# Silu as one ScalarE instruction, an early table load, folded ALiBi distances and moved tile addresses in a two-layer mLSTM and NSA decoder

## The chip, the core and the metric

The kernel runs on one NeuronCore of a Trainium2 chip. A core has engines that each run their own queue of instructions in order: TensorE (PE in the profile; its weight loads are PEld), VectorE (DVE), ScalarE (ACT), GpSimd (POOL) and SyncE (SP, which here only issues DMAs). They meet through semaphores. The metric is device microseconds of one execution; three executions of the kernel before took 578.73, 580.31 and 580.7 us, so its time is the median, 580.31 us.

## The reference

All data are float32; a sequence of 256 tokens, width 1024, two layers. Layer A is an mLSTM, layer B attends sparsely over keys and values that are computed once between the layers.

```python
def mlstm_mixer(h, w_in, conv_w, conv_b, w_q, w_k, w_v, w_gate, b_gate, head_norm, skip, w_out):
    xm, o_pre, z = jnp.split(h @ w_in, 3, axis=-1)          # 1024 -> 3 x 2048
    xc = jax.nn.silu(causal_depthwise_conv(xm, conv_w, conv_b))   # 4 taps
    q, k, v = blockdiag(xc, w_q), blockdiag(xc, w_k), blockdiag(xm, w_v)   # 512 blocks of 4 x 4
    gates = q @ w_gate[:2048] + k @ w_gate[2048:4096] + v @ w_gate[4096:] + b_gate
    cell = mlstm_cell(heads(q), heads(k), heads(v), i_pre, f_pre)    # 4 heads of 512
    hc = sigmoid(heads(o_pre)) * cell
    hn = per-head layer norm of hc, times head_norm
    return ((hn + skip * xc) * silu(z)) @ w_out

def nsa_mixer(h, kv, w_in, w_out):        # 16 heads of 128 in 2 groups, 3 branches
    q = (h @ w_q) * 128 ** -0.5
    s = q @ k.T - slopes[head] * distance     # masked where distance < 0
    p = masked_softmax(s, mask)               # for each of the 3 branches
    o = sum over branches of sigmoid(gate) * silu(z_branch) * (p @ v)
    return o @ w_out

x = x + rmsnorm(mixer(rmsnorm(x, g_pre)), g_post)      # for both layers
```

The three branches are the compressed blocks (15 of them, computed by a small MLP), the selected blocks and the window; at 256 tokens the last two see all earlier tokens.

## The kernel before, in words

The kernel is written for a framework that works out each engine's order when the program is built, from the order of the code, priorities (`high_priority`) and explicit hints (`issue_after(ins)`, meaning that an instruction is put behind `ins` on its engine). Tiles come from pools with a fixed number of buffers, and an instruction that needs a buffer still in use waits.

*Products in three passes.* Each float32 operand is split into a high part, a copy rounded to `fp32r`, and a low part, the rest. `split` makes the high part on ScalarE (L134, `whi<-raw`) and the low part on VectorE (L135, `wlo<-raw,whi`). `mm3` issues three matmuls: high x high, high x low, low x high (L139 to L141); the third is the one that needs the low half of the weights. `weights` (L117 and after) loads a tile of 128 x 1024 weights by a DMA from SP's queue (L123) into `raw` (4 buffers) and splits it into `whi` (5 buffers) and `wlo` (4). `proj_t` multiplies two such tiles with the normalised input `hA` (layer A) or `hB` (layer B); it gives a transposed result of 256 features by 256 tokens.

*Layer A up to the gates (some 12 to 95 us).* The loop at L364 goes over j = 0 to 7, 256 features each. In each turn it runs `proj_t` into `xmps`, copies it to `xm` (L373, ScalarE), starts the convolution with the fourth tap and the bias on ScalarE (`conv`, L378), adds three taps for each of the two feature tiles on VectorE (L381, six instructions), and applies Silu as conv * (1 + tanh(conv / 2)): Tanh on ScalarE (`th`, L384), then one VectorE instruction (`xc`, L385). The factor 0.5 that is missing so far, `xc` being twice the Silu, is put into its users: the gate weights (L354), the scores (L504: 0.25), the vector that holds `skip` (L305: 0.25 instead of 0.5). Between the projections stand quarters of the output gates (`o_gate`, L322). In the turns j = 4 and 5 `gate_product` (L345 to L354) makes the weights `wgt` of the gates, products of the 4 x 4 blocks with the gate matrix. Then `gps2` and `gps` (L398 and after) give the gates from `xm` and `xc`, and a chain of small steps on 4 rows follows, among them Abs, Exp and Ln on ScalarE (L421 to L423).

*Cells.* `block_product` (L356 to L360, called at L560) makes M, the blocks of w_q times w_k transposed. `cell_scores` expands the blocks to 128 x 128 tiles `bd` on GpSimd (L472), which wait for M; it makes the scores and the values `v`. `z_gate`, `cell_out` and `cell_y` follow for each head, then the output projection `OutProj` (its sums are `acc`; the weight tiles of its last steps are `wl`).

*Keys and values, and layer B (250 us to the end).* `wv` holds weights of the values; `dist` (L647 and after) holds the distances of every query to every key of all branches, MASKED = 1e33 where a key is not seen. Then heads run in pairs, p = 0 to 7: `q_proj` (L809) scales q and splits it; `softmaxes` (L817) makes `al` = -slope * dist on GpSimd (L825, one pass over 128 x 800 per head), scores on TensorE (`sps`), then on VectorE score + `al` with the row maximum (L838), the negated maximum `nm` (L841), and on ScalarE Exp with that bias (L846). `z_branch` makes silu(z) of a branch from `zps`; `transposes` turns the softmax results (`pt`, and `ptc` for the compressed branch, L886); `values` (L903) multiplies them with the values and writes y, for the pairs 0 to 3 into `ylow`, a tile that uses the buffer of a former input, for the others into tiles of the pool `yp`. The second `OutProj` ends the program.

Of the kernel before, what the change touches and what calls it, by code (L numbers as in the profile page):

```python
# [7 lines left out]
F32 = mybir.dt.float32  # L8
# [7 lines left out]
P = 128  # L16
# [4 lines left out]
def trunk(ctx: ExitStack, tc: tile.TileContext, x, norm_pre, norm_post, a_w_in, a_conv_w, a_conv_b,  # L21
# [171 lines left out]
    def new_hT(name):  # L193
        return [hp.tile([P, KT, S], F32R, tag="h8", name=f"{name}_{s}") for s in ("hi", "lo")]
# [51 lines left out]
    with ExitStack() as actx:  # L246
# [5 lines left out]

        NF = AI // P
# [22 lines left out]
        with tc.issue_after(last_pow[0].ins):  # L276
# [28 lines left out]
            nc.vector.tensor_scalar(vec[:, 96:112], vps[:, 96:112], 0.25, None, op0=ALU.mult)  # L305
# [39 lines left out]
        def gate_product(a):  # L345

            terms = ((wq_row, wg[0]), (wk_row, wg[1])) if a == 0 else ((blk[:, 1], wg[2]),)
            pr = ys.tile([P, NF, 2 * AH, len(terms), 4], F32, tag="y4", name=f"prod{a}")
            for i, (r, w) in enumerate(terms):
                nc.vector.tensor_mul(pr[:, :, :, i, :], rows(r, 2 * AH), w.rearrange("p t (j c) -> p t c j", j=4))  # L350
            dst = wgt[:, a, :, 0:2 * AH]
            nc.vector.tensor_reduce(dst, pr, axis=AX.XY if len(terms) > 1 else AX.X, op=ALU.add)
            if a == 0:
                nc.vector.tensor_scalar(dst, dst, 0.5, None, op0=ALU.mult)  # L354
# [9 lines left out]
        for j in range(NF // 2):  # L364
            if j > 1:
                next(og[(j - 2) // 4])
            with ExitStack() as st:
                if j > 0:
                    st.enter_context(tc.issue_after(last_mm[0]))
                ps = proj_t(a_w_in[0], j * 256, hT, "xmps")  # L370
            hold.clear()
            h, j0 = divmod(2 * j, HT)
            nc.scalar.activation(xm[h][:, j0:j0 + 2, 3:], ps, AF.Copy)  # L373
            acc = a2.tile([P, 2, S], F32, tag="conv", name="conv")
            for m in range(2):
                f = 2 * j + m
                src = xm[h][:, j0 + m, :]
                nc.scalar.activation(acc[:, m, :], src[:, 3:], AF.Identity, scale=vec[:, 48 + f:49 + f],  # L378
                                     bias=vec[:, 64 + f:65 + f])
                for k in range(3):  # L380
                    nc.vector.scalar_tensor_tensor(acc[:, m, :], src[:, k:k + S], vec[:, 16 * k + f:16 * k + f + 1],  # L381
                                                   acc[:, m, :], op0=ALU.mult, op1=ALU.add)
            th = a2.tile([P, 2, S], F32, tag="th", name="th")
            nc.scalar.activation(th, acc, AF.Tanh, scale=0.5)  # L384
            nc.vector.scalar_tensor_tensor(xc[h][:, j0:j0 + 2, :], th, 1.0, acc, op0=ALU.add, op1=ALU.mult)  # L385
            if j in (4, 5):
                gate_product(j - 4)
        next(og[1])
# [80 lines left out]
        def cell_scores(h):  # L469
# [34 lines left out]
            nc.vector.scalar_tensor_tensor(dd, sps, 0.25 * ADH ** -0.5, dd, op0=ALU.mult, op1=ALU.mult)  # L504
# [55 lines left out]
        block_product()  # L560
# [24 lines left out]
        for c in range(4):  # L585
# [7 lines left out]
            vch.append([a.rearrange("p (k n) -> p k n", k=2) for a in hl])  # L593
        hK = new_hT("hK")
# [27 lines left out]
    with ExitStack() as bctx:  # L622
# [25 lines left out]
        for c0, base in ((0, 0), (P + NB, 0), (W0, 0), (W0 + P, P), (W0 + 2 * P + NB, P), (W0 + 3 * P + NB, 0)):  # L648
            seg = dist[:, c0:c0 + P]
            nc.gpsimd.iota(seg, pattern=[[-1, P]], base=base, channel_multiplier=1,  # L650
                           allow_small_or_imprecise_dtypes=True)
            if base == 0:
                nc.gpsimd.affine_select(out=seg, in_=seg, pattern=[[-1, P]], compare_op=ALU.is_ge,
                                        fill=MASKED, base=0, channel_multiplier=1)
        for c0, base in ((P, 0), (W0 + 2 * P, P)):
            seg = dist[:, c0:c0 + NB]
            nc.gpsimd.iota(seg, pattern=[[-16, NB]], base=base, channel_multiplier=1,
                           allow_small_or_imprecise_dtypes=True)
            nc.gpsimd.tensor_scalar(seg, seg, -15.5, None, op0=ALU.add)
            nc.gpsimd.affine_select(out=seg, in_=seg, pattern=[[-16, NB]], compare_op=ALU.is_ge,  # L660
                                    fill=MASKED, base=base - 31, channel_multiplier=1)
# [147 lines left out]
        def q_proj(p):  # L809
            ps = proj_t(bw, p * 256, hB, "qps")  # L810
            q = [qz.tile([P, 2, S], F32R, tag=f"q{s}", name=f"q{s}{p}") for s in ("hi", "lo")]
            sc = float(DK) ** -0.5
            nc.scalar.activation(q[0], ps, AF.Copy, scale=sc)
            nc.vector.scalar_tensor_tensor(q[1], ps, sc, q[0].bitcast(F32), op0=ALU.mult, op1=ALU.subtract)
            return q

        def softmaxes(p, q):  # L817
# [3 lines left out]
            for j in range(2):  # L821
                h = 2 * p + j
                al = b2.tile([P, W0 + KW], F32, tag="al", name=f"al{h}")
                with tc.issue_after(after_norm):
                    nc.gpsimd.tensor_scalar(al, dist, -slopes[h], None, op0=ALU.mult)  # L825
                e = E[:, j, :]
                mx = col(6, "mx")
                for t in range(NT):
# [7 lines left out]
                    for b, (c0, n) in enumerate(segs[t]):  # L836
                        src = next(s[:, c0 - o:c0 - o + n] for o, w, s in where if o <= c0 < o + w)
                        nc.vector.tensor_tensor_reduce(e[:, c0:c0 + n], src, al[:, c0:c0 + n], 1.0, -1e30,  # L838
                                                       ALU.add, ALU.max, mx[:, 3 * t + b:3 * t + b + 1])
                nm = col(6, "nm")  # L840
                nc.vector.tensor_scalar(nm, mx, -1.0, None, op0=ALU.mult)  # L841
                sm = col(6, "sm")
                for t in range(NT):
                    for b, (c0, n) in enumerate(segs[t]):
                        i = 3 * t + b
                        nc.scalar.activation(e[:, c0:c0 + n], e[:, c0:c0 + n], AF.Exp, bias=nm[:, i:i + 1],  # L846
                                             accum_out=sm[:, i:i + 1])
# [55 lines left out]
        def values(p, pts, zz):  # L903
            ptc, pt0, pt1 = pts
            g = p // 4
            if p < 4:
# [63 lines left out]
        yp = bctx.enter_context(tc.tile_pool(name="yp", bufs=8, reuse_waits="tile"))  # L970
        ylow = [hp.tile([P, 4, 2, S], F32R, tag="h8", name=f"ylow{s}") for s in ("hi", "lo")]
# [60 lines left out]
```

## Time and profile before

| | |
|---|---|
| three executions | 578.73, 580.31, 580.7 us (median 580.31) |
| profiled execution | 581.31 us |
| its span in the trace | 579.5 us |
| granted TensorE clock over it | 0.998 |
| busy: TensorE, VectorE, ScalarE, GpSimd | 97%, 78%, 54%, 16% |
| time from turn to turn in layer B, per pair of heads | 28.5 us |

The rows that follow come from one execution, recorded by the hardware profiler. A busy share is an average over the whole program; where an engine stands still, and for whom, is read from the lists of waits and the timelines. A wait is put down to the event that ended last before the instruction began.

### The profile page before, as it was taken

What the parts mean: (1) busy time and instruction counts of PE and PEld (TensorE: products, weight loads), DVE (VectorE), ACT (ScalarE), POOL (GpSimd) and SP (SyncE); (2) the same over time, 40 slices, a digit from 0 to 9 for tenths busy, and PEclk for the clock granted to TensorE, in tenths of its full rate; (3) what the DMA queues carried; (4) which work ended last, traced back from release to release, by engine and by line L of the source; (5) the groups of instructions that cost most, each with busy time, mean ns of one, the idle gap of its engine ahead of it and who ended that gap; (6) DMA issues with size and microseconds to landing.
All of it is one profiled execution on the core that took longest, in us unless ns stands there. A gap on an engine that the chain in (4) does not pass through costs nothing.

```text
span 579.5 us, 10616 instructions
## 1 busy us (share of the span) xinstructions
PE 563.6 (97%) x4043; PEld 511.6 (88%) x4043; DVE 451.1 (78%) x944; ACT 310.7 (54%) x585; POOL 90.1 (16%) x104
## 2 busy tenths in 40 slices
PE   7988999999999999999999999999999999999995
PEld 3977986898999988879899999999999999998884
DVE  7679887485898886777625789989978989998663
ACT  5464775545454435563424574747474747475521
POOL 7610000201020040130003112121211221200000
PEclk9999999999999999999999999999999999999999
DMA  8985664344314347779896553636374636354601
GB/s 262 223 246 177 218 192 140 107 146 146 114 48 131 112 156 241 224 261 280 265 316 162 164 152 109 182 111 182 110 182 110 183 110 185 108 189 150 198 8 74
DMA packets 82693, 96.69 MB, mean 167 GB/s; under 512 B 4811, under 2 KB 68449, under 8 KB 82642
## 3 DMA queue, kind: packets, MB, share of 16 engines
q1 hardware_dynamic: 81040, 92.48, 52.6%
q0 software_dynamic: 1600, 3.52, 2.8%
q8 instruction: 32, 0.52, 0.4%
q14 instruction: 19, 0.16, 0.1%
q10 hardware_dynamic: 2, 0.00, 0.0%
HBM read 94.94 MB, written 1.05 MB: 166 GB/s over the span
## 4 chain that ended last, share of the span: by engine, by line
PE 82%; DVE 8%; DMA 5%; ACT 2%; issue 2%; POOL 0%; DVEq 0%; POOLq 0%; ACTq 0%
PE zps L139 10%; PE zps L141 10%; PE zps L140 10%; PE acc L139 5%; PE acc L141 5%; PE acc L140 5%; DMA raw<-in_a_w_in_dram 5%; DVE wlo L135 3%; PE qps L139 3%; PE qps L141 3%; PE qps L140 3%; PE pt L871 2%; DVE conv L381 2%; PE o L139 1%; PE sps L501 1%
## 5 line engine op out<-in xcount | busy, mean ns | idle before, releaser
L135 DVE TENSOR_TENSOR wlo<-raw,whi 128x1024 fp32r<-128x1024 f32 x150 | 181.8, 1228 | 59.2 <-ACT whi L134 21.6
L134 ACT ACTIVATE whi<-raw 128x1024 fp32r<-128x1024 f32 x151 | 157.0, 1052 | 120.2 <-PE zps L140 26.3
L139 PE MATMUL zps<-hB_hi,whi 128*128 128x256 f32 x384 | 108.1, 281 | 0.0
L140 PE MATMUL zps<-hB_lo,whi 128*128 128x256 f32 x384 | 107.2, 279 | 0.0
L141 PE MATMUL zps<-hB_hi,wlo 128*128 128x256 f32 x384 | 107.1, 279 | 0.0
L825 POOL TENSOR_SCALAR al<-dist 128x800 f32<-128x800 f32 x16 | 42.4, 2648 | 206.5 <-DVE mx L838 157.0
L139 PEld LDWEIGHTS zps<-hB_hi,whi 128*128 128x128 f32 x384 | 72.2, 188 | 0.8 <-issue 0.4
L140 PEld LDWEIGHTS zps<-hB_lo,whi 128*128 128x128 f32 x384 | 72.2, 188 | 0.0
L141 PEld LDWEIGHTS zps<-hB_hi,wlo 128*128 128x128 f32 x384 | 72.2, 188 | 0.0
L846 ACT ACTIVATE e<-e,nm 128x16 f32<-128x16 f32 (+2 forms) x96 | 37.7, 394 | 18.4 <-DVE nm L841 18.4
L141 PE MATMUL xmps<-hA_hi,wlo 128*128 128x256 f32 x128 | 36.2, 283 | 5.6 <-DVE wlo L135 5.6
L139 PE MATMUL xmps<-hA_hi,whi 128*128 128x256 f32 x128 | 35.8, 280 | 0.3 <-ACT whi L134 0.3
L139 PE MATMUL zps<-hA_hi,whi 128*128 128x256 f32 x128 | 36.1, 282 | 0.0
L141 PE MATMUL zps<-hA_hi,wlo 128*128 128x256 f32 x128 | 35.9, 280 | 0.0
L140 PE MATMUL zps<-hA_lo,whi 128*128 128x256 f32 x128 | 35.8, 280 | 0.0
L141 PE MATMUL qps<-hB_hi,wlo 128*128 128x256 f32 x128 | 35.8, 279 | 0.0
L140 PE MATMUL qps<-hB_lo,whi 128*128 128x256 f32 x128 | 35.8, 279 | 0.0
L140 PE MATMUL xmps<-hA_lo,whi 128*128 128x256 f32 x128 | 35.7, 279 | 0.0
L139 PE MATMUL qps<-hB_hi,whi 128*128 128x256 f32 x128 | 35.7, 279 | 0.0
L141 PEld LDWEIGHTS xmps<-hA_hi,wlo 128*128 128x128 f32 x128 | 24.0, 188 | 6.7 <-DVE wlo L135 6.7
L139 PE MATMUL o<-whi,hA_hi 128*128 128x512 f32 x64 | 25.6, 400 | 0.0
L140 PE MATMUL o<-wlo,hA_hi 128*128 128x512 f32 x64 | 25.4, 397 | 0.0
(338 smaller groups left out, 1410.4 us busy)
## 6 DMA issues: line engine op xcount, KB each, us to landing
raw<-in_b_w_in_dram SPq DMA_DIRECT2D x64, 512.0 KB, 4.8
raw<-in_a_w_in_dram SPq DMA_DIRECT2D x48, 512.0 KB, 4.8
raw<-in_a_w_out_dram SPq DMA_DIRECT2D x16, 512.0 KB, 3.7
w<-in_cmp_w_dram SPq DMA_DIRECT2D x32, 256.0 KB, 6.5
raw<-in_b_w_out_dram SPq DMA_DIRECT2D x16, 512.0 KB, 3.6
raw<-in_kv_w_dram SPq DMA_DIRECT2D x8, 512.0 KB, 6.9
raw<-in_kv_w_dram SPq DMA_DIRECT2D x8, 256.0 KB, 3.1
x<-in_x_dram SPq DMA_DIRECT2D x4, 256.0 KB, 4.2
```

What stands on the lines that cost most here:

```text
L134: a = nc.scalar.activation(hi, src, AF.Copy)
L135: return a.ins, nc.vector.tensor_sub(lo, src, hi.bitcast(F32)).ins
L139: nc.tensor.matmul(dst, lhsT=l[0], rhs=r[0], start=start, stop=False)
L140: nc.tensor.matmul(dst, lhsT=l[0], rhs=r[1], start=False, stop=False)
L141: last_mm[0] = nc.tensor.matmul(dst, lhsT=l[1], rhs=r[0], start=False, stop=stop).ins
L381: nc.vector.scalar_tensor_tensor(acc[:, m, :], src[:, k:k + S], vec[:, 16 * k + f:16 * k + f + 1], acc[:, m, :], op0=ALU.mult, op1=ALU.add)
L501: nc.tensor.matmul(sps[:, 0:S], lhsT=kk[:, j, 0:P], rhs=xc[h][:, j, :], start=j == 0, stop=j == HT - 1)
L825: nc.gpsimd.tensor_scalar(al, dist, -slopes[h], None, op0=ALU.mult)
L846: nc.scalar.activation(e[:, c0:c0 + n], e[:, c0:c0 + n], AF.Exp, bias=nm[:, i:i + 1], accum_out=sm[:, i:i + 1])
L871: nc.tensor.transpose(dst, E[:, j, c0:c0 + P], ident)
```

## The change

It has six parts.

1. Silu becomes one ScalarE instruction (`AF.Silu`) that writes `xc` directly; `xc` is now the Silu itself, and the factors 0.5 and 0.25 in its users go.
2. Behind the last Silu a one-column Exp of a constant is issued, so that the table that the gates' Abs and Exp use is loaded there.
3. `block_product` is called in turn j = 6 of the convolution loop instead of ahead of the cells.
4. The distances are kept negated and unscaled. q is divided by the head's slope when it is scaled (so each head of a pair has its own factor, and `q_proj` has two instructions each on ScalarE and VectorE, of half the width). One VectorE instruction computes -slope * (score / slope - distance), the negated score, with a row minimum in place of the maximum, and Exp has the scale -1. The GpSimd pass `al` and the negation of the maximum go.
5. `ylow` holds three pairs instead of four and starts 56 floats into its buffer; `yp` has 10 buffers.
6. Four pad tiles or offsets (`pad_y`, `pad_wv`, `pad_yT`, and the 56 floats) move addresses.

```diff
+        ap.tile([P, 104], F32, name="pad_y")
...
-            nc.vector.tensor_scalar(vec[:, 96:112], vps[:, 96:112], 0.25, None, op0=ALU.mult)
+            nc.vector.tensor_scalar(vec[:, 96:112], vps[:, 96:112], 0.5, None, op0=ALU.mult)
...
-            if a == 0:
-                nc.vector.tensor_scalar(dst, dst, 0.5, None, op0=ALU.mult)
...
-            th = a2.tile([P, 2, S], F32, tag="th", name="th")
-            nc.scalar.activation(th, acc, AF.Tanh, scale=0.5)
-            nc.vector.scalar_tensor_tensor(xc[h][:, j0:j0 + 2, :], th, 1.0, acc, op0=ALU.add, op1=ALU.mult)
+            silu = nc.scalar.activation(xc[h][:, j0:j0 + 2, :], acc, AF.Silu)
             if j in (4, 5):
                 gate_product(j - 4)
+            if j == 6:
+                block_product()
+            if j == NF // 2 - 1:
+
+                with tc.issue_after(silu.ins):
+                    nc.scalar.activation(col(2, "ss")[:, 0:1], mhalf[:, 0:1], AF.Exp)
...
-            nc.vector.scalar_tensor_tensor(dd, sps, 0.25 * ADH ** -0.5, dd, op0=ALU.mult, op1=ALU.mult)
+            nc.vector.scalar_tensor_tensor(dd, sps, ADH ** -0.5, dd, op0=ALU.mult, op1=ALU.mult)
...
-        block_product()
...
+        wv.tile([P, 120], F32, tag="pad", bufs=1, name="pad_wv")
...
-            sc = float(DK) ** -0.5
-            nc.scalar.activation(q[0], ps, AF.Copy, scale=sc)
-            nc.vector.scalar_tensor_tensor(q[1], ps, sc, q[0].bitcast(F32), op0=ALU.mult, op1=ALU.subtract)
+            for j in range(2):
+                sc = float(DK) ** -0.5 / slopes[2 * p + j]
+                nc.scalar.activation(q[0][:, j, :], ps[:, j, :], AF.Copy, scale=sc)
+                nc.vector.scalar_tensor_tensor(q[1][:, j, :], ps[:, j, :], sc, q[0][:, j, :].bitcast(F32),
+                                               op0=ALU.mult, op1=ALU.subtract)
...
-                al = b2.tile([P, W0 + KW], F32, tag="al", name=f"al{h}")
-                with tc.issue_after(after_norm):
-                    nc.gpsimd.tensor_scalar(al, dist, -slopes[h], None, op0=ALU.mult)
...
-                        nc.vector.tensor_tensor_reduce(e[:, c0:c0 + n], src, al[:, c0:c0 + n], 1.0, -1e30,
-                                                       ALU.add, ALU.max, mx[:, 3 * t + b:3 * t + b + 1])
-                nm = col(6, "nm")
-                nc.vector.tensor_scalar(nm, mx, -1.0, None, op0=ALU.mult)
+
+                        nc.vector.tensor_tensor_reduce(e[:, c0:c0 + n], src, dist[:, c0:c0 + n], -slopes[h], 1e30,
+                                                       ALU.add, ALU.min, nm[:, 3 * t + b:3 * t + b + 1])
...
                         nc.scalar.activation(e[:, c0:c0 + n], e[:, c0:c0 + n], AF.Exp, bias=nm[:, i:i + 1],
-                                             accum_out=sm[:, i:i + 1])
+                                             scale=-1.0, accum_out=sm[:, i:i + 1])
...
-            if p < 4:
+            if p < 3:
...
-        yp = bctx.enter_context(tc.tile_pool(name="yp", bufs=8, reuse_waits="tile"))
-        ylow = [hp.tile([P, 4, 2, S], F32R, tag="h8", name=f"ylow{s}") for s in ("hi", "lo")]
+        yp = bctx.enter_context(tc.tile_pool(name="yp", bufs=10, reuse_waits="tile"))
+        yp.tile([P, 8], F32, tag="pad", bufs=1, name="pad_yT")
+        ylow = [hp.tile([P, 4 * 2 * S], F32R, tag="h8", name=f"ylow{s}")[:, 56:56 + 3 * 2 * S].rearrange(
+            "p (q i s) -> p q i s", q=3, i=2) for s in ("hi", "lo")]
```

The addresses as the two programs are built, within a partition and modulo 64 bytes: the weight tiles `whi` and `wlo` lie at 32 in both; the inputs `hA`, `hK`, `hB` at 0 in both; y, `yT` and `ylow` at 0 before and 32 after; v at 0 before and 32 after, where the score tiles `sd` that it is multiplied with are at 32; `wv` at 32 before and 0 after; the last weight tiles `wl` of layer A's output projection at 0 in both.

The orders that follow are those of the built programs; a row is an engine's instruction with its line, operation, tiles and shape. First VectorE in the convolution loop, before, in the turns where the gate weights are made: `wlo` is the low half of a weight tile, `conv` a step of the convolution, `prod` and `wgt` belong to the gate weights.

```order
L135 TENSOR_TENSOR wlo_605<-raw_602,whi_604 128x1024
L381 SCALAR_TENSOR_TENSOR conv<-xm_238,vec,conv 128x256
L354 TENSOR_SCALAR wgt<-wgt 128x16x8
L350 TENSOR_TENSOR prod_775<-blk,wg_217 128x512
L385 SCALAR_TENSOR_TENSOR xc_241<-th,conv 128x512
L135 TENSOR_TENSOR wlo_611<-raw_608,whi_610 128x1024
L135 TENSOR_TENSOR wlo_683<-raw_680,whi_682 128x1024
L352 TENSOR_REDUCE wgt<-prod_775 128x16x8
L381 SCALAR_TENSOR_TENSOR conv<-xm_238,vec,conv 128x256 x6
L135 TENSOR_TENSOR wlo_705<-raw_702,whi_704 128x1024
```

And the same place in the changed program, where `prod_m` and the reduction to `blk` are the two instructions of `block_product`:

```order
L135 TENSOR_TENSOR wlo_598<-raw_595,whi_597 128x1024
L381 SCALAR_TENSOR_TENSOR conv<-xm_239,vec,conv 128x256
L352 TENSOR_TENSOR prod_763<-blk,wg_218 128x512
L135 TENSOR_TENSOR wlo_604<-raw_601,whi_603 128x1024
L354 TENSOR_REDUCE wgt<-prod_763 128x16x8
L135 TENSOR_TENSOR wlo_673<-raw_670,whi_672 128x1024
L359 TENSOR_TENSOR prod_m<-wq_blk,qk_row 128x256
L381 SCALAR_TENSOR_TENSOR conv<-xm_239,vec,conv 128x256
L360 TENSOR_REDUCE blk<-prod_m 128x64
L381 SCALAR_TENSOR_TENSOR conv<-xm_239,vec,conv 128x256 x4
L135 TENSOR_TENSOR wlo_695<-raw_692,whi_694 128x1024
```

The scaling of `wgt` and `xc` are gone from between the weight tiles, the reduction of the gate weights has moved up between two of them, and M's two instructions stand among the convolution steps behind.

ScalarE around the gates, before: `whi` is the high half of a weight tile, `grows` are the four rows of gates.

```order
L134 ACTIVATE whi_1212<-raw_1210 128x1024
L384 ACTIVATE th<-conv 128x512
L421 ACTIVATE grows_1044<-grows_1044 4x256
L422 ACTIVATE grows_1044<-grows_1044 4x256
L423 ACT_TABLE_LOAD
L423 ACTIVATE grows_1044<-grows_1044,ones 4x256
```

And after; the lines of the gates have moved by four.

```order
L134 ACTIVATE whi_1198<-raw_1196 128x1024
L383 ACTIVATE xc_243<-conv 128x512
L391 ACT_TABLE_LOAD
L391 ACTIVATE ss<-mhalf 128x1
L425 ACTIVATE grows_1033<-grows_1033 4x256
L426 ACTIVATE grows_1033<-grows_1033 4x256
L427 ACT_TABLE_LOAD
L427 ACTIVATE grows_1033<-grows_1033,ones 4x256
```

A table load and the one-column Exp (L391) have come in behind the last Silu (L383). At the first Silu, ScalarE has another load that was not there before; Tanh used the table that was loaded at the start. Before:

```order
L134 ACTIVATE whi_426<-raw_424 128x1024
L384 ACTIVATE th<-conv 128x512
L134 ACTIVATE whi_493<-raw_491 128x1024
L134 ACTIVATE whi_512<-raw_510 128x1024
L373 ACTIVATE xm_237<-xmps 128x2x256
```

After:

```order
L134 ACTIVATE whi_423<-raw_421 128x1024
L383 ACT_TABLE_LOAD
L383 ACTIVATE xc_242<-conv 128x512
L134 ACTIVATE whi_488<-raw_486 128x1024
L134 ACTIVATE whi_507<-raw_505 128x1024
L373 ACTIVATE xm_238<-xmps 128x2x256
```

Silu stands where Tanh stood, and the load ahead of it.

## Rows read from the trace of the kernel before

**Rows 1.** The page, busy us, share of the span and instructions of each engine

```profile
PE 563.6 (97%) x4043; PEld 511.6 (88%) x4043; DVE 451.1 (78%) x944; ACT 310.7 (54%) x585; POOL 90.1 (16%) x104
```

**Rows 2.** TensorE's waits, whole span: releaser, us in all, times, longest

```profile
PE xmps L141 <- DVE wlo L135: 5.6, 5, 2.0
...
PE oc L912 <- DVE ptc L886: 0.3, 1, 0.3
```

**Rows 3.** Timeline of TensorE: start us, us, instruction, idle before it

```profile
41.99 0.39 PE L141 MATMUL xmps<-hA_hi,wlo 128*128 128x256 f32 x1 [2.01 <-DVE wlo L135]
...
49.47 0.38 PE L141 MATMUL xmps<-hA_hi,wlo 128*128 128x256 f32 x1 [0.21 <-DVE wlo L135]
...
52.81 0.38 PE L141 MATMUL xmps<-hA_hi,wlo 128*128 128x256 f32 x1 [1.66 <-DVE wlo L135]
```

**Rows 4.** Timeline of VectorE, convolution loop and M

```profile
37.22 2.18 DVE L381 SCALAR_TENSOR_TENSOR conv<-xm,vec,conv 128x256 f32<-128x256 f32 x5
...
40.10 0.69 DVE L385 SCALAR_TENSOR_TENSOR xc<-th,conv 128x512 f32<-128x512 f32 x1 [0.70 <-ACT th L384]
...
49.71 0.23 DVE L354 TENSOR_SCALAR wgt<-wgt 128x128 f32<-128x128 f32 x1
49.85 1.17 DVE L350 TENSOR_TENSOR prod<-blk,wg 128x512 f32<-128x512 f32 x1
50.92 0.69 DVE L385 SCALAR_TENSOR_TENSOR xc<-th,conv 128x512 f32<-128x512 f32 x1
51.53 2.36 DVE L135 TENSOR_TENSOR wlo<-raw,whi 128x1024 fp32r<-128x1024 f32 x2
...
103.41 0.41 DVE L359 TENSOR_TENSOR prod_m<-wq_blk,qk_row 128x256 f32<-128x256 f32 x1
```

**Rows 5.** Timeline of TensorE, one z product in three successive pairs

```profile
398.76 0.37 PE L139 MATMUL zps<-hB_hi,whi 128*128 128x256 f32 x1
...
427.27 0.37 PE L139 MATMUL zps<-hB_hi,whi 128*128 128x256 f32 x1
...
456.95 0.37 PE L139 MATMUL zps<-hB_hi,whi 128*128 128x256 f32 x1
```

**Rows 6.** Timeline of ScalarE at the first Silu and at the gates

```profile
28.96 0.62 ACT L384 ACTIVATE th<-conv 128x512 f32<-128x512 f32 x1
...
31.00 1.06 ACT L134 ACTIVATE whi<-raw 128x1024 fp32r<-128x1024 f32 x1 [1.42 <-DMA raw<-in_a_w_in_dram]
...
95.40 1.28 ACT L423 ACT_TABLE_LOAD   x1
96.70 0.51 ACT L423 ACTIVATE grows<-grows,ones 4x256 f32<-4x256 f32 x1
```

**Rows 7.** Waits of TensorE's weight loads, 52 to 92 us

```profile
PEld gps L398 <- DVE xc L385: 0.5, 1, 0.5
```

**Rows 8.** Groups by line: busy us, mean ns, idle before and releasers

```profile
L825 POOL TENSOR_SCALAR al<-dist 128x800 f32<-128x800 f32 x16 | 42.4, 2648 | 206.5 <-DVE mx L838 157.0 <-PE R L723 49.5
...
L841 DVE TENSOR_SCALAR nm<-mx 128x6 f32<-128x6 f32 x16 | 10.5, 655 | 0.1
```

**Rows 9.** Groups by form, TensorE's output projection

```profile
L139 PE MATMUL acc<-whi,yhi 128*128 128x512 f32 x56 | 22.5, 401 | 0.0
...
L140 PE MATMUL acc<-wlo,yhi 128*128 128x512 f32 x56 | 22.2, 396 | 0.0
...
L139 PE MATMUL acc<-wl,yhi 128*128 128x512 f32 x8 | 3.2, 394 | 0.0
```

**Rows 10.** ScalarE's waits, 28 to 54 us

```profile
ACT whi L134 <- DMA raw<-in_a_w_in_dram: 4.9, 3, 2.0
```

**Rows 11.** Waits of SP's DMA queue, 28 to 92 us

```profile
SPq L123 <- DVE wlo L135: 56.9, 22, 7.3
```

**Rows 12.** Timeline of VectorE at 29 us

```profile
29.09 2.17 DVE L135 TENSOR_TENSOR wlo<-raw,whi 128x1024 fp32r<-128x1024 f32 x1 [0.99 <-ACT whi L134]
```

**Rows 13.** Timeline of GpSimd at 29 us

```profile
29.13 1.04 POOL L472 TENSOR_TENSOR bd<-blk,bm 128x512 f32<-128x512 f32 x1
```

More of the change, by code (lines that the diff above doesn't have):

```diff
@@ L649, in trunk @@
             seg = dist[:, c0:c0 + P]
-            nc.gpsimd.iota(seg, pattern=[[-1, P]], base=base, channel_multiplier=1,
+            nc.gpsimd.iota(seg, pattern=[[1, P]], base=-base, channel_multiplier=-1,
                            allow_small_or_imprecise_dtypes=True)
@@ L653, in trunk @@
                 nc.gpsimd.affine_select(out=seg, in_=seg, pattern=[[-1, P]], compare_op=ALU.is_ge,
-                                        fill=MASKED, base=0, channel_multiplier=1)
+                                        fill=-MASKED, base=0, channel_multiplier=1)
         for c0, base in ((P, 0), (W0 + 2 * P, P)):
             seg = dist[:, c0:c0 + NB]
-            nc.gpsimd.iota(seg, pattern=[[-16, NB]], base=base, channel_multiplier=1,
+            nc.gpsimd.iota(seg, pattern=[[16, NB]], base=-base, channel_multiplier=-1,
                            allow_small_or_imprecise_dtypes=True)
-            nc.gpsimd.tensor_scalar(seg, seg, -15.5, None, op0=ALU.add)
+            nc.gpsimd.tensor_scalar(seg, seg, 15.5, None, op0=ALU.add)
             nc.gpsimd.affine_select(out=seg, in_=seg, pattern=[[-16, NB]], compare_op=ALU.is_ge,
-                                    fill=MASKED, base=base - 31, channel_multiplier=1)
+                                    fill=-MASKED, base=base - 31, channel_multiplier=1)
         hsel = bp.tile([6 * NB, 2], F32, name="hsel")
@@ L822, in softmaxes @@
                 h = 2 * p + j
-                al = b2.tile([P, W0 + KW], F32, tag="al", name=f"al{h}")
-                with tc.issue_after(after_norm):
-                    nc.gpsimd.tensor_scalar(al, dist, -slopes[h], None, op0=ALU.mult)
                 e = E[:, j, :]
-                mx = col(6, "mx")
+                nm = col(6, "nm")
                 for t in range(NT):
```

## The prediction

> **What bounds the kernel now.** I read the page first: TensorE is busy 563.6 of 579.5 us [rows 1], so the order of its matmuls is the program's length, and a change can only give back time in which it stands still, or make its matmuls themselves faster or slower. So the second view is the list of what TensorE waited for over the whole span: the largest entry by far is the projection of the convolution's input, 5.6 us in five waits, all for VectorE's low half of a split weight tile; a wait of 0.3 us for `ptc` follows in the softmax loop [rows 2]. Third, the timeline of TensorE at that projection: three of the five waits, 2.01, 0.21 and 1.66 us, lie between 39 and 53 us [rows 3], 3.88 us in all. Fourth, the timeline of VectorE there [rows 4]. It shows what stood ahead of the late weight tiles: at 40.10 the last step of the old Silu (`xc`, 0.69 us), which itself waited 0.70 us for ScalarE's Tanh; and at 49.71 to 50.92 the scaling of the gate weights (0.23), their product (1.17) and another `xc` (0.69), after which the two weight tiles come at 51.53. VectorE is the bound in this stretch, and TensorE stands behind it.
>
> In the softmax loop I looked at when TensorE starts the third z product of a pair of heads: 398.76, 427.27, 456.95 [rows 5]. The first distance is 28.51 us, the second 29.68: one pair took 1.17 us more than its neighbour, with the same matmuls.
>
> **The change part by part, against the profiled execution's own 581.31 us** (span 579.5 and 1.8 around it). It is 1.0 us above the median of the three runs shown, 580.31.
>
> *Silu as one ScalarE instruction.* VectorE loses eight `xc` instructions of 0.69 us, ScalarE keeps one instruction of the same shape in Tanh's place. In the order the late weight tile now follows the five convolution steps directly. These end at 37.22 + 2.18 = 39.40; the tile before started where `xc` ended, 40.10 + 0.69 = 40.79; consecutive rows on VectorE start about 0.1 us before the end of the one before, in both cases. So it starts 1.39 us earlier, and TensorE's first wait falls from 2.01 to 0.62. Ten microseconds later the scaling is gone (49.85 - 49.71 = 0.14 from start to start) and `xc` (51.53 - 50.92 = 0.61): 0.75 us more, which comes off the wait of 1.66. The wait of 0.21 between them stays, since both sides have moved by 1.39. Sum on TensorE: 1.39 + 0.75 = 2.14 us, inside the 3.88 there is to win.
>
> *What the new instruction costs.* No row shows a Silu. Its bounds are the nearest shapes on ScalarE: nothing more than the Tanh it replaces (0.62 [rows 6]), or at worst the whole weight tile's 1.06 us, twice as many elements. I take 0.62, the same shape and operands. At the upper end each of the four Silus in the stretch delays the weight tile behind it by 0.44; VectorE meets these tiles late anyway, so at most the 0.44 of the last one counts.
>
> *Tables.* There are two loads more: Silu's before the first Silu, and Exp's after the last one. A load is 1.28 us, and the instruction behind it started 96.70 - 95.40 = 1.30 after it began. The first falls at 28.96, where ScalarE's next weight tile starts only at 31.00, after 1.42 us of waiting for its DMA [rows 6]: 28.96 + 1.30 + 0.62 = 30.88, so the DMA covers it, by 0.12. Without that cover it would cost 1.3 on ScalarE. The second falls between the last Silu and the gates' first ScalarE instruction, where ScalarE idles. Cost 0 each. The Trainium skill, page "ScalarE: Activation LUTs", section "What ACT_TABLE_LOAD costs", states about 1283 ns for the load and about 1380 ns of draining, 2.66 us in all. The first half agrees with the row; the second does not show there. By the page's figure the first load would end the Silu at 32.24 and hold ScalarE up by 1.24, an estimate of up to 579.0 for the whole.
>
> *The gates.* TensorE's weight loads waited 0.5 us for the last `xc` [rows 7]. Silu's result is there 0.7 us earlier, so the wait goes; part of it may meet the next thing that chain waits for, so the bounds are 0 and 0.5; I count 0.2, nearer to the lower end. Behind it the chain of small gate steps starts that much earlier, and TensorE's next meeting with it, the four transposes now in one row, moves with it: 0.
>
> *Blocks' M with xm.* The product, 0.41 us, and its sum, a second instruction that I take as long, leave 103.41 [rows 4] for the convolution steps behind the weight tiles of 51.53: 0.8 us. TensorE's wait at 52.81 is for the first of these tiles and the last of the five; both new instructions stand behind the second, ahead of the next one after it, for which TensorE did not wait. That slack is the cover: 0. Without it they cost 0.8. At the old place they were nobody's wait either.
>
> *Distances.* GpSimd loses 16 passes of 2.65 us, VectorE 16 negations of 0.66 [rows 8]; the low half of q becomes two instructions, which by the shapes of [rows 4] (two of 2.18 / 5 = 0.44 for one of 0.69) adds 0.2 per pair. Per pair VectorE sheds 2 x 0.66 - 0.2 = 1.1 us. In an ordinary pair TensorE does not wait for it, so this gives nothing. In the long pair it does: there the 1.17 us came from `ptc` arriving late on VectorE, and with 1.1 us less queued ahead that is absorbed. I count 1.1 in this execution. The median runs, 1.0 us shorter, probably had little of it.
>
> *Places modulo 64 bytes.* 444 matmuls of 512 columns (168 and 192 of the two output projections, 36 with v, 48 with the K/V weights) get both operands at the same place; 24 that had it lose it. The trace has both kinds side by side: `acc<-wl` with both operands at 0 takes 394 ns; with y at 0 and weights at 32, `acc<-wlo` takes 396 and `acc<-whi` 401 [rows 9]. Bounds: 444 x 7 ns = 3.1 us won (401 - 394), and, from the pair that lies nearer, 444 x 2 = 0.9 lost, should same places at 32 turn the sign. 396 and 401 differ by more than 396 and 394 though their places are the same, so the place is not what parts them: I take 0.
>
> Sum: 581.31 - 2.14 - 0.2 - 1.1 = 577.9; from the median, without the long pair, 580.31 - 2.34 = 578.0. I forecast **577.9 us**.
>
> **Rivals.** *The time is given back to DMA.* TensorE comes earlier, but the weights do not. For: between 28 and 54 us ScalarE waited 4.9 us for weight transfers, three times [rows 10], and these waits stand ahead of the ones I remove. Against: from 28 to 92 us the queue that issues the loads waited 56.9 us for VectorE to release a raw tile [rows 11]; so a faster VectorE also issues them earlier. If half of the 2.14 goes this way, and the long pair stays a matter of luck: 580.31 - 1.07 - 0.2 = 579.0; I put it at 579.3.
>
> *The made-earlier M collides.* A VectorE weight tile at 29.09 took 2.17 us [rows 12], where two together take 2.36 at 51.53, about 1.2 each; and just then GpSimd ran a block expansion from 29.13 for 1.04 us [rows 13]. With M made at 52, GpSimd's next expansion follows it at about 53.5, in the middle of the convolution steps, and can hold VectorE for the same 2.17 - 1.2 = 0.95 us. With M's 0.8 that is 1.75 us ahead of the next weight tiles, of which no row gives the slack; if 0.95 of it shows on TensorE: 577.9 + 0.95 = 578.9. Against it: the order alone doesn't say that the two meet. The Trainium skill, page "SBUF — State Buffer", section "Who interferes with whom", says that a VectorE instruction with two SBUF inputs and a GpSimd one that reads SBUF exclude each other for the whole instruction; the pair of rows agrees.
>
> *The softmax loop begins to wait (slower).* The loop's order on ScalarE and VectorE is rewritten: exponentials are split by weight tiles, and the halves of q stand between the transposes' copies. If `ptc` then comes late in every pair as it did in the long one, each of the seven turns costs 1.17: 577.9 + 1.1 + 8.2 = 587.2. It decides the sign from (2.3 + 1.7) / 7 = 0.6 us per turn. For it: the one wait for `ptc` in the list shows how near the edge it is. Against: VectorE has 1.1 us less per pair ahead of it, and in six of seven turns there is no wait at all.
>
> *The places speed up TensorE.* At the upper bound of 3.1 us: 574.8. For it speaks only the row of 401, against it the one of 396.
>
> **How the numbers follow.** Two measurements of this kernel can be told apart from about 0.3%, 1.7 us: faster means under 578.6, slower over 582.0. Forecast 0.60 (nine tenths of it under 578.6), given back to DMA 0.19 (mostly within), collision 0.07 (mostly within), loop waits 0.08 (slower), places 0.06 (faster). Faster: 0.54 + 0.02 + 0.02 + 0.06 = 0.64; slower 0.08; the same 0.28. Range: the lower end takes all of the 3.88, 0.5 at the gates and 0.4 of luck in the runs off the median, 575.5; the upper end is the rival of DMA with nothing won, 580.3. Outside lie the loop that waits and part of the faster places.
>
> **What would show it.** Right: TensorE's waits between 39 and 53 us are about 0.6, 0.2 and 0.9; no wait for `xc` at the gates; the load of Silu's table ends before 31.0; distances between turns of the loop all 28.5. Wrong: the waits are the same length but start earlier, and end on a DMA; or `zps` steps of the loop drift apart; or matmuls of `acc` that differ from 396 ns.

## The result and the profile after

The changed kernel takes 574.53 us (median of 5 runs, 574.06 to 574.97), the kernel before in the same session 580.11. The ratio is 0.9912, 95% interval 0.9898 to 0.9926: 5.1 us faster. The direction was right and the size was not: the time lies 1.0 us under the lower end of the range. The profiled execution took 574.73 us, with a span of 573.0.

The page after, in the columns of [rows 1], and the whole list of TensorE's waits that answers to [rows 2]:

```profile
PE 558.3 (97%) x4043; PEld 511.5 (89%) x4043; DVE 438.4 (77%) x927; ACT 316.8 (55%) x596; POOL 52.4 (9%) x88
```

```profile
PE xmps L141 <- DVE wlo L135: 2.5, 2, 1.6
PE nT L188 <- DVE nrm L185: 2.0, 2, 1.1
PE spare L104 <- DVE ones_b L96: 1.8, 1, 1.8
PE vps L303 <- DMA rows<-in_a_skip_dram: 0.7, 1, 0.7
PE kcps L754 <- DVE hid L750: 0.5, 1, 0.5
PE vps L141 <- DVE hK_lo L135: 0.2, 1, 0.2
```

TensorE waits 3.1 us less for `wlo`, and the wait for `ptc` is gone; new are one of 0.5 us for `hid`, and more waiting at the start. But TensorE's busy time itself fell by 5.3 us, with the same 4043 matmuls. 2.1 us of that lies in the first 12.8 us, where busy and idle time trade places (10.37 us busy in the window of before, 8.28 after); most of the rest has to be matmuls that take less time.

The timeline of TensorE, where three waits stood in [rows 3], now has one between 39 and 53 us; ahead of it, VectorE and ScalarE at the place of [rows 4] (the tile behind the five convolution steps) and of [rows 6] (the first Silu):

```profile
49.98 0.38 PE L141 MATMUL xmps<-hA_hi,wlo 128*128 128x256 f32 x1 [0.91 <-DVE wlo L135]
```

```profile
36.59 2.19 DVE L381 SCALAR_TENSOR_TENSOR conv<-xm,vec,conv 128x256 f32<-128x256 f32 x5
38.69 1.22 DVE L135 TENSOR_TENSOR wlo<-raw,whi 128x1024 fp32r<-128x1024 f32 x1
```

```profile
28.09 1.28 ACT L383 ACT_TABLE_LOAD   x1
29.38 0.63 ACT L383 ACTIVATE xc<-conv 128x512 f32<-128x512 f32 x1
30.12 1.06 ACT L134 ACTIVATE whi<-raw 128x1024 fp32r<-128x1024 f32 x1
```

The weight tile follows the convolution steps at once. Silu takes 0.63 us, as Tanh took 0.62. The load ahead of it takes 1.28, and Silu starts 1.29 after the load began. The drain, the second half of the figure of the Trainium skill ("ScalarE: Activation LUTs", section "What ACT_TABLE_LOAD costs"), doesn't show here either.

The output projection of layer A by form, which answers to [rows 9]:

```profile
L139 PE MATMUL acc<-whi,yhi 128*128 128x512 f32 x56 | 22.1, 395 | 0.0
L140 PE MATMUL acc<-wlo,yhi 128*128 128x512 f32 x56 | 21.9, 390 | 0.0
```

401 has become 395, and 396 has become 390: 6 ns for each matmul whose operands got the same place. The Trainium skill ("Perfetto Trace Analysis", section "Tensor Engine Instruction (MATMUL, LD_WEIGHTS)") says that the end of a TensorE instruction is estimated and not measured. The trace agrees, as these matmuls of 390 to 401 ns start every 227 to 234 ns. So below a matmul's price is its step, from its start to the next one's, with steps over 300 ns (waits, other work) left out. Two operands are at the same place when their addresses within a partition are equal under the modulus that is spoken of.

### The profile page after: what moved, and what is told of

Its sections match the earlier page's. It is cut to its first block, busy times and chain, and to the rows that moved or that the text cites. A ratio compares the mean times of both kernels' runs of the same rounds, so it can differ in the third digit from the quotient of the medians.

```text
span 573.0 us, 10564 instructions
## 1 busy us (share of the span) xinstructions
PE 558.3 (97%) x4043; PEld 511.5 (89%) x4043; DVE 438.4 (77%) x927; ACT 316.8 (55%) x596; POOL 52.4 (9%) x88
## 4 chain that ended last, share of the span: by engine, by line
PE 84%; DMA 7%; DVE 4%; ACT 1%; issue 1%; SPq 1%; POOL 0%; DVEq 0%; POOLq 0%; ACTq 0%
PE zps L139 10%; PE zps L141 10%; PE zps L140 10%; PE acc L139 5%; PE acc L140 5%; PE acc L141 5%; DMA raw<-in_b_w_in_dram 4%; PE o L139 3%; PE o L140 2%; PE o L141 2%; PE xmps L141 2%; PE qps L139 2%; PE qps L141 2%; PE qps L140 2%; PE xmps L139 2%; PE xmps L140 2%
## 5 line engine op out<-in xcount | busy, mean ns | idle before, releaser
L163 POOL TENSOR_TENSOR r<-u,mhalf 128x1 f32<-128x1 f32 x8 | 4.5, 562 | 350.8 <-DVE u L173 350.8
L381 DVE SCALAR_TENSOR_TENSOR conv<-xm,vec,conv 128x256 f32<-128x256 f32 x48 | 21.0, 479 | 6.3 <-ACT conv L378 6.2
```

The costliest lines, as they stand in the source:

```text
L163: last_pow[0] = nc.gpsimd.tensor_tensor(r, u, mhalf[:, 0:n], op=ALU.pow)
```

## The experiments

Times are medians of runs; each kernel was timed beside the kernel before (medians 579.59 with e1 to e4, 580.06 with e5 and e6, 579.78 in the one run with e7 to e9, 580.26 with e10 to e12), and ratios are to it.

**e1, the changed kernel without the places.** The pads, `ylow` and `yp` are as before.

```diff
-        ap.tile([P, 104], F32, name="pad_y")
...
-        wv.tile([P, 120], F32, tag="pad", bufs=1, name="pad_wv")
...
-            if p < 3:
+            if p < 4:
...
```

> The changed kernel without part 5 and 6 (pads, ylow and yp as before, so the addresses of before). Theory: the start-to-start time of a 512-column matmul whose two operands got the same place fell from 233.4 to 227.6 ns in the trace, 444 of them, so without the places it takes 574.5 + 2.6 = 577.1 us, and acc and vps matmuls step by 233 ns again. Rival (the places do nothing, as the forecast had it, and the gain is all from Silu, M and the distances): 574.5 us.

576.12 us, ratio 0.9939 (0.9921 to 0.9956): between the two, nearer to the theory. The rows are those of before again:

```profile
L139 PE MATMUL acc<-whi,yhi 128*128 128x512 f32 x56 | 22.5, 401 | 0.0
L140 PE MATMUL acc<-wlo,yhi 128*128 128x512 f32 x56 | 22.2, 396 | 0.0
```

So are the steps: 355 of the matmuls of the two output projections take 82.94 us from start to start, as before, and 80.80 in the trace after.

**e2, Silu, early Exp and M alone, and e3, the same with M at its old place.** Both have the addresses and the distances of before. The two lines with `j == 6` are in e2 alone.

```diff
-            th = a2.tile([P, 2, S], F32, tag="th", name="th")
-            nc.scalar.activation(th, acc, AF.Tanh, scale=0.5)
-            nc.vector.scalar_tensor_tensor(xc[h][:, j0:j0 + 2, :], th, 1.0, acc, op0=ALU.add, op1=ALU.mult)
+            silu = nc.scalar.activation(xc[h][:, j0:j0 + 2, :], acc, AF.Silu)
...
+            if j == 6:
+                block_product()
...
```

> The kernel before with parts 1 to 3 alone (Silu, early Exp, M with xm); addresses and distances of before. Theory: the whole convolution stretch is won, 4.2 us of TensorE waits less, and 0.7 at the gates: 575.2 to 576.0 us, and no VectorE weight tile of over 2 us at 28 us. Rival (the recorded sum, only what stood directly ahead of the late tiles goes): 577.8 us.

> As e2, but M is made where it was before, ahead of the cells. Theory: GpSimd's first block expansion runs at 29 us again, as in the trace of before, where it lies beside a VectorE weight tile of 2.17 us; in the changed kernel it waits until M is made. So the tile is slow again and it takes 0.9 us more than e2. Rival (the place of M decides nothing, cost 0 as recorded): the time of e2 within 0.3 us.

e2 takes 577.10 us, ratio 0.9950 (0.9931 to 0.9969), 2.9 us less than before (1.8 to 4.0); e3 577.07, 0.9952 (0.9933 to 0.9971). So the recorded sum for Silu holds, the theory of 4.2 does not, and M's place is worth nothing that can be measured. The waits of TensorE from 39 to 53 us in e2:

```profile
PE xmps L141 <- DVE wlo L135: 1.7, 3, 0.9
```

```profile
40.94 0.38 PE L141 MATMUL xmps<-hA_hi,wlo 128*128 128x256 f32 x1 [0.53 <-DVE wlo L135]
...
48.45 0.39 PE L141 MATMUL xmps<-hA_hi,wlo 128*128 128x256 f32 x1 [0.20 <-DVE wlo L135]
...
51.06 0.38 PE L141 MATMUL xmps<-hA_hi,wlo 128*128 128x256 f32 x1 [0.94 <-DVE wlo L135]
```

The prediction left 0.62 + 0.21 + 0.91 = 1.74 us in three waits; here are 1.7 in three, and each of them is near its forecast. In e3 they are 1.4 together. That M decides by way of a collision fell too. In e3 GpSimd's expansion stands at 29.50 for 1.04 us, as in [rows 13], and it meets no weight tile, because those come at other times in this execution (25.14 and 30.82):

```profile
25.14 1.22 DVE L135 TENSOR_TENSOR wlo<-raw,whi 128x1024 fp32r<-128x1024 f32 x1 [1.26 <-PE xmps L141]
26.28 2.61 DVE L379 SCALAR_TENSOR_TENSOR conv<-xm,vec,conv 128x256 f32<-128x256 f32 x6
30.82 1.23 DVE L135 TENSOR_TENSOR wlo<-raw,whi 128x1024 fp32r<-128x1024 f32 x1 [1.93 <-ACT whi L134]
```

The theory of 4.2 us came from comparing one trace of before with one of after. e1 and e2 have the same order up to layer B, and still their profiles stand 1.9 us apart at 48 us. A single pair of traces can't price a stage that begins with transfers.

**e4, the distances alone.**

```diff
...
-                    nc.gpsimd.tensor_scalar(al, dist, -slopes[h], None, op0=ALU.mult)
...
-                nc.vector.tensor_scalar(nm, mx, -1.0, None, op0=ALU.mult)
...
```

> The kernel before with part 4 alone (distances kept, q divided by the slope, no pass on GpSimd, no negation). Theory: the long pair's waits (0.9 us in the traces compared) go, and a new wait of 0.5 us for hid at about 305 us comes, from the halved instructions of the first q: 579.7 us. Rival (recorded): 1.1 less than the profiled execution and no new wait, 579.0 to 579.2; second rival: the long pair was chance, and with the new wait it is 580.6.

579.00 us, ratio 0.9991 (0.9976 to 1.0005): some 0.5 us, not clear of nothing. The traces say more. From the first `oc` matmul of a pair to the next pair's (in us; the last one holds the output projection too):

```
before  28.51 28.51 28.98 29.20 28.50 28.50 34.08
e2      28.51 28.51 28.54 29.10 28.50 28.50 34.08
e3      28.50 28.51 28.51 28.90 28.50 28.50 34.08
e4      28.51 28.51 28.51 28.50 28.50 28.50 34.08
after   28.56 28.51 28.51 28.50 28.50 28.50 33.41
```

All three executions without the new distances have a long turn, 0.4 to 1.2 us in all; both with them have none, and in e1, e5 and e10 to e12, which have them too, the turns ahead of the last lie between 28.50 and 28.56. Since e4 takes out GpSimd's pass and VectorE's negation together, it isn't shown which of the two did it. The new wait for `hid` is 0.5 us in the changed kernel's first profile, and e4's list of waits doesn't have it: it comes and goes.

**e5, which place counts.** The y of three pairs is moved on by different amounts. The other operand, the weights, stays.

```diff
+        for s, shift in (("hi", (16, 32, 64)), ("lo", (8, 24, 128))):     # floats
+            a = hp.tile([P, 4 * 2 * S], F32R, tag="h8", name=f"ylow{s}")
+            ylow.append([a[:, 56 + q * 2 * S + d:56 + (q + 1) * 2 * S + d].rearrange("p (i s) -> p i s", i=2)
+                         for q, d in enumerate(shift)])
...
```

> The changed kernel with the y of the pairs 0, 1, 2 moved apart from the weights' place: the high halves by 64, 128 and 256 bytes, the low halves by 32, 96 and 512. Read from the starts of consecutive matmuls acc<-ylow of 512 columns. Theory 'same place modulo 64': 227.6 ns wherever the high half is at 64, 128 or 256, 233.4 only where the low half is at 32 or 96. Theory 'modulo 128' (for which speaks that acc<-wl, 64 apart modulo 128, stepped by 233.4 in the kernel before): 64 is slow too, 128 and 256 are fast. Theory 'modulo 512': all but the low half of pair 2 are slow. The time itself 574.5 to 575.

The timeline of TensorE in pair 0 (the high half 64 bytes off), three matmuls to a product; the last row is the first matmul of the fourth product:

```profile
519.64 0.39 PE L139 MATMUL acc<-whi,ylowhi 128*128 128x512 f32 x1
519.88 0.40 PE L140 MATMUL acc<-wlo,ylowhi 128*128 128x512 f32 x1
...
521.73 0.40 PE L139 MATMUL acc<-whi,ylowhi 128*128 128x512 f32 x1
```

(521.73 - 519.64) / 9 = 232 ns a step. Median steps in ns of the 24 matmuls of each pair, by the bytes that the operand is off:

| pair | high half off | whi, yhi | wlo, yhi | low half off | whi, ylo |
|---|---|---|---|---|---|
| 0 | 64 | 235 | 232 | 32 | 236 |
| 1 | 128 | 233 | 234 | 96 | 232 |
| 2 | 256 | 227 | 227 | 512 | 226 |

64 and 128 are slow, 256 and 512 are fast. For these matmuls "the same place" means the same modulo 256 bytes; none of the three theories had that number. The one run of e5, 577.07 us, says nothing on a term of this size.

**e10, the same modulo 64 but not modulo 256, e11, the changed kernel beside it, and e12, the changed kernel without the early Exp.**

```diff
-        ap.tile([P, 104], F32, name="pad_y")
+        ap.tile([P, 120], F32, name="pad_y")
...
-        wv.tile([P, 120], F32, tag="pad", bufs=1, name="pad_wv")
+        wv.tile([P, 104], F32, tag="pad", bufs=1, name="pad_wv")
...
-        yp.tile([P, 8], F32, tag="pad", bufs=1, name="pad_yT")
-        ylow = [hp.tile([P, 4 * 2 * S], F32R, tag="h8", name=f"ylow{s}")[:, 56:56 + 3 * 2 * S].rearrange(
+        yp.tile([P, 24], F32, tag="pad", bufs=1, name="pad_yT")
+        ylow = [hp.tile([P, 4 * 2 * S], F32R, tag="h8", name=f"ylow{s}")[:, 72:72 + 3 * 2 * S].rearrange(
```

And the edit of e12:

```diff
-            if j == NF // 2 - 1:
-
-                with tc.issue_after(silu.ins):
-                    nc.scalar.activation(col(2, "ss")[:, 0:1], mhalf[:, 0:1], AF.Exp)
```

> The changed kernel with y, yT, ylow, v and wv moved on by 64 bytes (16 floats more or less in each pad): still the same place as the other operand modulo 64, no longer modulo 256. Theory 'modulo 256' (from e5, where 64 and 128 were slow and 256 fast): the 444 matmuls step by 233 ns again, 2.6 us more than the changed kernel: 577.1 us, as e1. Rival 'modulo 64', as the change's description has it: the time of the changed kernel, 574.5.

> The changed kernel itself, beside e10 and e12 on the same chip, so that the price of the places is read from runs of one session: 574.5 us; the difference to e10 2.6 us if all 444 matmuls lie on the path, 1.6 if the difference to e1 was the true one.

> The changed kernel without the one-column Exp behind the last Silu, so that Exp's table (1.28 us a load) is loaded inside the chain of gate steps. Theory (the early load costs nothing and the gates' chain has little slack): 0 to 1.3 us slower, 0.3 to 0.5 likely. Rival (TensorE never waits for that chain): no difference, 574.5 us.

e10: 577.09 us, ratio 0.9948 (0.9929 to 0.9968). e11: 575.16, ratio 0.9911 (0.9889 to 0.9933). Their difference is 1.9 us, and the fastest run of e10 (576.45) is slower than the slowest of e11 (575.73): modulo 64 is not enough. Unlike e1, e10 leaves the pools as they are in the changed kernel and moves addresses alone. The steps give the same sum: in e10 the 355 recorded steps of the two output projections take 82.75 us, in e11 80.80, 1.95 less, and those of `vps` 0.08 less. `num` and `vps`, which e10 puts 192 bytes apart, step by 230 there, `num` no slower than in e11 (where its operands have the same place and it steps by 230 as well), so e10 gives back a little less than the whole. Between the traces of before and after these sums are 2.1 for the projections, 0.1 for `num` and 0.2 for `vps`: 2.5 us in all.

e12: 575.57 us, ratio 0.9921 (0.9898 to 0.9944), 0.4 above e11 and not clear of it. Its trace shows where the load went: into the chain of gate steps, for whose end TensorE then waits 0.7 us.

```profile
PE tps L449 <- ACT grows L441: 0.5, 1, 0.5
PE tps L449 <- DVE grows L427: 0.2, 1, 0.2
```

**e6, the inputs h at the weights' place as well.** If the rule holds for every matmul, 2500 more of them gain.

```diff
-    tp.tile([P, 72], F32, tag="pad", bufs=1, name="pad_h")
-    sp.tile([P, 56], F32, tag="pad", bufs=1, name="pad_s")
+    tp.tile([P, 128], F32, tag="pad", bufs=1, name="pad_h")
...
```

> The changed kernel with the normalised inputs hA, hK, hB moved to the weights' place too (the pad of 56 floats goes from one pool to the one ahead of the inputs, so nothing else moves; ylow begins at its buffer's start, wv's pad is 64 floats). Theory (what counts is that both operands of a matmul lie at the same place, whatever its columns): the 256-column matmuls of all projections, some 2500, step by 113.8 instead of 116.7 ns, 7.2 us, and the 192 of the output gates and 24 of wl by 227.6 instead of 233.4, 1.25 us: 574.5 - 8.5 = 566.0 us. Rival 1 (the 256-column matmuls have another limit): 573.3. Rival 2 (TensorE is faster, but waits for weight tiles take half of it back): 570.

580.91 us, ratio 1.0014 (0.9997 to 1.0031): the whole gain is lost. The group of z products, of after and then of e6 (there a line has gone above it):

```profile
L139 PE MATMUL zps<-hB_hi,whi 128*128 128x256 f32 x384 | 108.1, 282 | 0.0
```

```profile
L138 PE MATMUL zps<-hB_hi,whi 128*128 128x256 f32 x384 | 109.5, 285 | 0.0
```

Matmuls of 512 columns gained as expected (output gates 227 instead of 234 ns at the median). Those of 256 columns, with the weights as the stationary operand, went the other way, from 116.7 to 119.9 ns a step: some 2490 of them take 300.7 us instead of 293.2 in e11. In those of 512 columns the weights are the moving operand, so it isn't shown whether the width or the roles turn the sign.

**e7 to e9, other places for h.** The buffers of h are 64 bytes longer (e7), the same and 32 bytes further on (e8), or 32 bytes longer (e9), so that the halves stand at different places. The diff is that of e7; the other two also change the pads ahead of h.

```diff
-        ylow = [hp.tile([P, 4 * 2 * S], F32R, tag="h8", name=f"ylow{s}")[:, 56:56 + 3 * 2 * S].rearrange(
+        ylow = [hp.tile([P, 4 * 2 * S + 16], F32R, tag="h8", name=f"ylow{s}")[:, 56:56 + 3 * 2 * S].rearrange(
```

> The changed kernel with the buffers of the inputs h 64 bytes longer, so that hA's high half stands 224 bytes behind the weights modulo 256 (weights minus h), its low half 32, hB's halves 96 and 32. Read from the starts of consecutive 256-column matmuls. Theory A (for 256 columns the same place alone is bad, 119.9 ns, every other place gives 116.7): 116.7 everywhere, time that of the changed kernel within 1 us. Theory B (256 columns have a good place as 512 have, only elsewhere): one of 224, 32, 96 steps by 113.8 or less.

> As e7, all 32 bytes further: hA's halves at 192 and 0, hB's at 64 and 0. Theory A: 119.9 ns for the low halves at 0, 116.7 for 192 and 64; about 1.0 + 2.4 x 0.5 us slower than e7. Theory B: 192 or 64 steps by 113.8 or less.

> As e7 with buffers 32 bytes longer: hA's halves at 224 and 128, hB's at 160 and 128. Theory A: 116.7 ns everywhere. Theory B: 160 or 128 steps by 113.8 or less.

Mean steps in ns of the z products of layer B (three matmuls to a product, steps over 150 ns left out; after and e6 for comparison), by weights minus h in bytes modulo 256:

| run | place of h's high half | whi, high | wlo, high | place of the low half | whi, low |
|---|---|---|---|---|---|
| after | 224 | 116.9 | 116.6 | 224 | 116.8 |
| e6 | 0 | 119.9 | 119.8 | 0 | 119.8 |
| e7 | 96 | 117.1 | 117.8 | 32 | 120.7 |
| e8 | 64 | 119.9 | 117.4 | 0 | 119.2 |
| e9 | 160 | 118.4 | 118.2 | 128 | 119.8 |

Theory B falls: no place tried comes to 113.8. Theory A falls as well: other places than the same one are slow too. 224, where h already stood, is the best of those seen; 192 (the high half in layer A in e8) steps by 116.7 to 118.0. The single runs of 579.41, 579.66 and 578.51 us lie 4.0 to 5.1 us above the changed kernel's 574.53, where theory A had e7 within 1 us of it and e8 2.2 above e7. Where the halves lie at different places it isn't shown which of two neighbouring 256-column matmuls pays. For 512 columns there is a hint: as the programs are built, the longer buffers move `ylow` too, in e7 its high half to 64 bytes off the weights, while its low half stays at their place. There `whi, ylo`, whose own operands agree, steps by 234.5 ns and is followed by a `yhi` that is 64 off, while `wlo, yhi`, itself 64 off and followed by a `ylo` in place, steps by 230.3; in e9, with 32 off, it is 233.5 and 230.6. So a step goes with the place of the y that comes next at least as much as with that of its own; why isn't shown. The output gates alone gained in e6 (42.71 us for 187 recorded steps instead of 43.64 in e11); weight tiles of their own at hA's place might give that 0.9 us without the loss. This wasn't run, and no version beat the changed kernel.

## Why the prediction was wrong, point by point

- *Silu.* Right in mechanism and size. 2.14 of 3.88 us was forecast, with 1.74 left in three waits; e2 shows 0.53, 0.20 and 0.94 where 0.62, 0.21 and 0.91 were to be left. With the gates (0.2) the part was forecast at 2.34, and e2 measured 2.9 (1.8 to 4.0).
- *What Silu costs, and the tables.* Right in the cost, 0.63 us against 0.62 taken and nothing for the loads, but the cover of the first load was another. The prediction hid it in a wait of ScalarE for a transfer. In the trace after, ScalarE's next weight tile follows Silu at once (Silu ends at 30.01, the tile starts at 30.12), and VectorE waits for it:

```profile
31.22 1.23 DVE L135 TENSOR_TENSOR wlo<-raw,whi 128x1024 fp32r<-128x1024 f32 x1 [1.58 <-ACT whi L134]
```

TensorE, however, waits for nothing between 15 and 49 us there, so the slack is its own. (The prediction's estimate by the figure of the Trainium skill, "ScalarE: Activation LUTs", adds up to 577.9 + 1.24 = 579.1, not 579.0.) The second load is hidden where it was put: it ends at 89.03 in the trace after and the gates' first step on ScalarE begins at 91.08; left out (e12), TensorE waits 0.7 us. The wait for `xc` at the gates of [rows 7] is gone in the trace after; in those of e1 and e2 0.3 of its 0.5 us is left.

- *Blocks' M.* Cost 0, right: e2 and e3 are within 0.03 us. The meeting that the rival of a collision feared did take place, but GpSimd lost by it, not VectorE. In the trace after, the expansion behind the early M takes 5.08 us beside VectorE's work, where [rows 13] has 1.04, while the weight tiles that VectorE makes within it take their usual 1.21:

```profile
52.80 5.08 POOL L476 TENSOR_TENSOR bd<-blk,bm 128x512 f32<-128x512 f32 x1 [21.14 <-DVE blk L360]
```

```profile
54.23 1.21 DVE L135 TENSOR_TENSOR wlo<-raw,whi 128x1024 fp32r<-128x1024 f32 x1
55.37 0.47 DVE L381 SCALAR_TENSOR_TENSOR conv<-xm,vec,conv 128x256 f32<-128x256 f32 x1
55.76 1.21 DVE L135 TENSOR_TENSOR wlo<-raw,whi 128x1024 fp32r<-128x1024 f32 x1
```

TensorE has no wait for GpSimd, so this costs nothing. Nor was the slow tile of [rows 12] a matter of one execution: beside the same expansion at 29 us, e4 has an `xc` of 1.53 us instead of 0.69. There VectorE loses.

```profile
29.39 1.13 POOL L472 TENSOR_TENSOR bd<-blk,bm 128x512 f32<-128x512 f32 x1
```

```profile
29.53 1.53 DVE L385 SCALAR_TENSOR_TENSOR xc<-th,conv 128x512 f32<-128x512 f32 x1
```

- *Distances.* The long turns go, as forecast; that it is VectorE's lighter queue that does it is argued, not shown. Of the 1.17 us that the prediction put down to `ptc`, the list of waits of before names 0.3 for `ptc` and 0.2 for `yacc`. 1.1 us was counted in the profiled execution and nothing in the median; e4 has 0.5 (1.4 less to 0.3 more), and other executions had long turns too, of 0.4 and 0.6 us.
- *Places.* **This step failed.** "I take 0", between bounds of 0.9 lost and 3.1 won; e11 against e10 is 1.9 us won, and the steps of the traces 2.5. The step rested on `acc<-wl` at 394 ns as a pair with the same place. It isn't one. In the built program y lies at 64 modulo 256 and `wl` at 0: they are the same modulo 64, but 64 apart modulo 256, and by e5 that is as slow as any. So the comparison in [rows 9] set a slow pair beside a slow pair, and found them alike. Their steps would have said so at once: 233.4 ns for `acc<-wl` and 233.6 for the others in the trace of before, while the 394 to 401 are durations with an estimated end. The description's modulus was taken over, and nothing in the trace tested it.
- *The rivals.* "The places speed up TensorE" was the right one, at 574.8 us, and had a chance of 0.06, because only one row spoke for it. That its time lies 0.3 us from the measured one is in part luck: it counts 3.1 us for the places, where 1.9 to 2.5 were measured, and 1.1 for the distances, where e4 has 0.5. No time was seen to go back to DMA or to a loop that waits, and the collision cost TensorE nothing.

Together: Silu and gates 2.9, distances 0.5, places 1.9 make 5.3 us; 580.11 - 574.53 is 5.6, and 0.9912 of the time of before is 5.1 less. Counted from the median before, the forecast had 2.3 of these. No part is left over that could be told from noise. The parts' own intervals (about 1 us each) are wide enough that the shares of Silu and of the places could shift by half a microsecond against each other.

## What to carry to other kernels

When a change moves addresses, first look for a pair of rows that truly differ in what the change alters, under each modulus that it could mean; a comparison that shows no difference may be between two of the same kind. Price matmuls by the step from start to start, since a few per cent of 444 of them (2.5 us) can be as much as the largest entry in a list of waits. And price a stage that begins with transfers from several executions or from a kernel with that part alone.

## What was not expected of the hardware

- In these runs the step of the 512-column fp32r matmuls of the projections depends on how the operands' addresses stand to each other modulo 256 bytes: 227 ns at the same place, 230 to 236 at the others in e1, e5 and e10. `num` is an exception, with 230 at the same place. For 256 columns with stationary weights the same place is bad (119.8 against 116.8).
- In the profiled execution of the changed kernel TensorE stood still for 1.57 us up to 14.92 us, and in the window from 12.8 to 20 us it had a granted clock of 0.76, where before, e1, e2 and e11 have 1.00. e6 stood still for 1.46 us at the same matmul and kept 1.00, so what lowered the clock isn't shown. The matmuls of 256 columns stepped by 0.22 us there, nearly twice the 0.117 of later, as at the lower of the two levels (1.2 GHz). The columns of the second fence are TensorE busy, loads, VectorE, ScalarE, GpSimd, then clock, DMA share and GB/s.

```profile
14.92 0.58 PE L141 MATMUL xmps<-hA_hi,wlo 128*128 128x256 f32 x1 [1.57 <-DVE wlo L135]
15.29 0.42 PE L139 MATMUL xmps<-hA_hi,whi 128*128 128x256 f32 x1
15.51 0.41 PE L140 MATMUL xmps<-hA_lo,whi 128*128 128x256 f32 x1
```

```profile
12.80:20.00 7.20, 5.62 (x33) 5.43 (x34) 5.13 (x8) 2.81 (x3) 5.52 (x10) 0.76 1.31 138
```

It did 33 matmuls there where e1 did 45, and by 28 us it was 1.5 us behind the trace of before. By 42 us it was 1.6 ahead: the late start came off later waits.
